# Queries before keys and values in a hybrid encoder layer, each query tile stored head by head, with the output projection's first operands loaded before the values

## The chip, the cores and the metric

One core of one Trainium2 chip runs the whole kernel. The core has a tensor engine (TensorE, PE in the profile; its weight loads are PEld), a vector engine (DVE), a scalar engine (ACT), a general engine (POOL) and a sync engine (SP), which here issues nearly all transfers. The metric is the device time of one execution in microseconds (us).

## The reference, cut to what matters

A two-layer encoder step. In each layer three groups of heads work on the same input: latent attention with 8 heads, an mLSTM with 4, a gated delta net with 4. Their outputs are gated, joined into 1536 mixed columns and projected back to 1024. A prompt of 16 + 1024 rows and 8 running streams of 16 rows each go through it, 1168 rows together. The change concerns the step between the input projection and the attention, where queries, keys and values are made from the normalised latents, and the beginning of the output projection.

```python
def mixer_layer(x, pos0, ...):
    proj = rms_norm(x, norm_w) @ w_in
    (c_q, c_kv, k_r, z_a, m_q, ...) = jnp.split(proj, ...)
    q = (rms_norm(c_q, q_norm) @ w_uq).reshape(B, L, MLA_HEADS, MLA_NOPE + MLA_ROPE)    # 8 heads of 64 + 32
    q_nope, q_rope = q[..., :MLA_NOPE], apply_rope(q[..., MLA_NOPE:], pos)
    c_new = rms_norm(c_kv, kv_norm)
    ...
    o_a = mla_attention(q_nope, q_rope, c_all, kr_all, w_uk, w_uv, ...)
    ...
    mixed = jnp.concatenate([o_a * jax.nn.silu(z_a), o_m * jax.nn.silu(z_m), o_g * jax.nn.silu(z_g)], axis=-1)
    return x + mixed @ w_out, ...

def mla_attention(...):
    k_nope = jnp.einsum('bkr,rhd->bkhd', c_kv, w_uk)
    v = jnp.einsum('bkr,rhd->bkhd', c_kv, w_uv)
    ...
        sc = jnp.einsum('blhd,bkd->bhlk', q_rope[:, s:e], k_rope[:, :n_keys])
        sc = sc + jnp.einsum('blhd,bkhd->bhlk', q_nope[:, s:e], k_nope[:, :n_keys])
        p = jax.nn.softmax(jnp.where(mask, sc * scale, -jnp.inf), axis=-1)
        o = jnp.einsum('bhlk,bkhd->blhd', p, v[:, :n_keys])
```

## The kernel before

**Number format.** A float32 product is made of three matmuls on a rounded high half and the remainder of each operand (`mm3`, L428 on). `split` makes the halves: a cast on ACT (line L421 in the trace), a subtraction on DVE or POOL in turn (L425). `weights` loads a weight tile through one buffer (`wf`) and splits it into one of two (`wh`).

**Memory.** Large tiles are pages, 28 buffers of 128 x 1200 float32 (`pg`, `free`); `room(n)` says whether n of them are free. PSUM has 3 buffers `pa`, for projections and transposes, and 5 `pb`, for scores and the rest. Small work tiles come from rings: "hp" has 3 buffers, "th" two. The "hp" ring is shared by the evicted queries and keys, by the loads of queries and keys for a head (`gload`) and by the loads of the mixed rows (`mixes`). Scratch for the queries (`qS`, 8 heads x 96 x 1168), the keys (`kS`, 4 pairs of heads x 128 x 1040) and the mixed rows (`mixS`, 12 x 128 x 1168) is in DRAM.

**Order of the work.** The program is written by generators that a planner (`Weave`) takes in turn, by a clock that it models from the matmuls (`W.t`). Threads (`prep`, `gload`, `att_s`, `att_t`, `att_fin`, and some for the running streams) yield a number, the microseconds after which they are due again, or a name, which they wait for. Where no thread is due and the pages suffice, the next step of a filler is written: input projection (`projs`), then `qkv`, `out_first`, `out_proj`. So the order on each engine is settled when the program is built; on the chip each engine takes its queue in that order, and waits there for what the next instruction needs. All loads and stores named here stand in SP's one queue, but for those of the rotary keys (`krS`), which POOL issues.

**The step in question.** `qkv` takes five weight tiles in the order keys, queries 0 and 1, values, queries 2 and 3, queries 4 and 5; the next tile is loaded when one is begun. Each query tile (27 matmuls) covers three slices of the 1168 rows, 400, 384 and 384. Tiles 0 and 3 hold the rotary parts of four heads each: DVE makes the products with the two tables (`tab`), one of 128 partitions (L1442) and two of 64 (L1445), POOL adds them. Tiles 1, 2, 4 and 5 hold the other 64 columns of two heads each and are scaled by ACT (L1451). Each slice is evicted into an "hp" buffer and stored from there, a rotary slice by two transfers [4 x 16 x 400], another by one [2 x 64 x 400]. Keys (12 pieces of 6 matmuls) are copied by ACT (L1425) into "hp" and stored piece by piece; values (9 tiles of 6) go to four pages by ACT and DVE in turn (L1411, L1414, L1415).

**Around it.** `gload` waits for `("spill", g)`, the queries and keys of a pair of heads, then loads a head's pieces back through "hp" and splits them (ACT L1506, POOL L1507). `att_s` makes scores and softmax (ACT L1553) for one head and 128 rows at a time, 9 such units per head in layer 0 and 8 in layer 1, at most four ahead of `att_t`, which transposes the weights (L356) and multiplies by the values. `out_first` starts the output projection with the first 4 of 12 mixed rows, which don't come from the attention: 24 slices of 12 matmuls, filler between the units. It loads the twelve operand pieces with `mixes`:

```python
        def mixes(k0, k1):
            mx = [(pg(F32R), pg(F32R)) for _ in range(k0, k1)]
            for s0, s1 in wsl:
                for k, (a, b_) in zip(range(k0, k1), mx):
                    t_ = wt("hp", 528, 3)[:, :s1 - s0]
                    ld(t_, mixS[k][:, s0:s1])
                    split(t_, a[:, s0:s1], b_[:, s0:s1])
            return mx
```

`wout` loads a weight tile of that projection (SP L1944 in one stretch, L437 in others). The matmuls themselves stand on L345, transposes on L356.

Of the kernel before, what the change touches and what calls it, by code (L numbers as in the profile page):

```python
# [294 lines left out]
def _build(nc, tc, ctx, I, O, layers):  # L295
# [275 lines left out]
    def layer(l, XH, XLp, XL, xres, xw, R):  # L571
# [795 lines left out]
        def qkv():  # L1367
# [7 lines left out]
            VV = A["VV"] = [pg() for _ in range(4)]  # L1375
            order = ["k", "q0", "v", "q1", "q2"]

            def load(i_):
                if i_ == len(order):
                    return None  # L1380
                t_ = order[i_]
                if t_ == "v":
                    return weights(I["wuv"][l].rearrange("p k c -> p (k c)"), 1024)
                if t_ == "k":
                    return weights(I["wuk"][l].rearrange("p g k c -> p (g k c)"), 1024)
                g = int(t_[1])
                return weights(I["wuq"][l, :, 2 * g:2 * g + 2].rearrange("p h k c -> p (h k c)"), 768)

            nxt = load(0)
            todo = [(i_, t_, j) for i_, t_ in enumerate(order)  # L1390
                    for j in {"v": (0,), "k": range(4)}.get(t_, [2 * (ord(t_[-1]) - 48), 2 * (ord(t_[-1]) - 48) + 1])]
            gr = 0
            ckn = []
            pre = -1
            for i_, t_, j in todo:
                if i_ != pre:
                    wh, wl = nxt
                    nxt = load(i_ + 1)
                    pre = i_
                if t_ == "v":  # L1400
                    for g in range(4):
                        gate(G.memset(VV[g][:, 1024:1152], 0.0))
                    for c in range(9):
                        ps = pa()
                        tc_ = slice(OFF[c], OFF[c] + 128)
                        for k in range(2):
                            mm3(ps, ckh[k][:, tc_], ckl[k][:, tc_], wh[:, 512 * k:512 * k + 512],
                                wl[:, 512 * k:512 * k + 512], k == 0, k == 1)
                        if c == 0:
                            for g in range(4):  # L1410
                                S.copy(VV[g][0:16, 1024:1152], ps[0:16, 128 * g:128 * g + 128])  # L1411
                        else:
                            o = 512 * ((c - 1) % 2)
                            (S.copy if c % 2 else V.tensor_copy)(VV[(c - 1) // 2][:, o:o + 512], ps)  # L1414
                        yield  # L1415
                elif t_ == "k":
                    w0 = 256 * j
                    for s0, s1 in KS:
                        ps = pa()
                        w = s1 - s0  # L1420
                        for k in range(2):
                            sl = slice(w0 + 128 * k, w0 + 128 * k + 128)
                            mm3(ps[:, :w], wh[:, sl], wl[:, sl], ckh[k][:, s0:s1], ckl[k][:, s0:s1], k == 0, k == 1)
                        t32 = wt("hp", 528, 3)
                        S.copy(t32[:, :w], ps[:, :w])  # L1425
                        QE.dma_start(kS[j][:, s0:s1], t32[:, :w])
                        yield
                else:
                    rope = j in (0, 3)
                    a = j // 3  # L1430
                    w0 = 384 * (j % 2)
                    for s0, s1 in SLICES:
                        ps = pa()
                        w = s1 - s0
                        for k in range(3):
                            sl = slice(w0 + 128 * k, w0 + 128 * k + 128)
# [564 lines left out]
```

## Time and profile before

| | |
|---|---|
| median of 3 runs | 2755.95 us (2751.81 to 4520.19) |
| the profiled execution's own time | 2758.32 us |
| its span in the trace | 2756.5 us |
| TensorE busy | 2570.4 us, 93% of the span, 18526 matmuls |
| DVE, ACT, POOL busy | 1524.6, 1181.5, 715.9 us |
| bytes moved, mean | 259.80 MB, 94 GB/s |

The span is the stretch from the first to the last instruction that the hardware profiler recorded; the execution's own time is 1.8 us longer. A busy matmul engine says that matmuls were in flight, not that they ran at the full clock: the granted clock stands apart, as a share of 2.4 GHz. Of the rows that a later section shows, each was taken from this one execution.

### The profile page before, as it was taken

What the parts mean: (1) busy time and instruction counts of PE and PEld (TensorE: products, weight loads), DVE (VectorE), ACT (ScalarE), POOL (GpSimd) and SP (SyncE); (2) the same over time, 40 slices, a digit from 0 to 9 for tenths busy, and PEclk for the clock granted to TensorE, in tenths of its full rate; (3) what the DMA queues carried; (4) which work ended last, traced back from release to release, by engine and by line L of the source; (5) the groups of instructions that cost most, each with busy time, mean ns of one, the idle gap of its engine ahead of it and who ended that gap; (6) DMA issues with size and microseconds to landing.
All of it is one profiled execution on the core that took longest, in us unless ns stands there. A gap on an engine that the chain in (4) does not pass through costs nothing. (4 is left out here: it accounts for less than half of the span.)

```text
span 2756.5 us, 48832 instructions
## 1 busy us (share of the span) xinstructions
PE 2570.4 (93%) x18526; PEld 2022.9 (73%) x18526; DVE 1524.6 (55%) x4280; ACT 1181.5 (43%) x2935; POOL 715.9 (26%) x803
## 2 busy tenths in 40 slices
PE   6999999999999689999999999999999976999997
PEld 4676777767767568879976767676776665788996
DVE  6568475564352255675566764756443413656746
ACT  4353444444442344464243534444443323545522
POOL 2223222122123232132341331222211322221414
PEclk9999999999999889999999999999999997999998
DMA  3212122221123243386422121212211333444852
GB/s 124 62 38 76 49 67 63 64 59 50 55 82 126 86 129 103 101 232 195 154 82 57 58 67 51 67 49 68 65 48 48 116 116 98 120 115 130 248 167 86
DMA packets 184538, 259.80 MB, mean 94 GB/s; under 512 B 50112, under 2 KB 143792, under 8 KB 184304
## 3 DMA queue, kind: packets, MB, share of 16 engines
q1 hardware_dynamic: 182576, 251.83, 30.7%
q0 software_dynamic: 1728, 4.86, 0.7%
q8 instruction: 146, 2.39, 0.4%
q14 instruction: 88, 0.72, 0.1%
HBM read 191.77 MB, written 64.86 MB: 93 GB/s over the span
## 5 line engine op out<-in xcount | busy, mean ns | idle before, releaser
L345 PE MATMUL pa<-pg,wh 128*128 128x384 f32 (+2 forms) x6324 | 1640.9, 391 | 44.3 <-ACT pg L421 17.6
L345 PEld LDWEIGHTS pa<-pg,wh 128*128 128x128 f32 x6324 | 1126.7, 196 | 84.3 <-issue 19.2
L345 PE MATMUL pa<-pg,wb 128*128 128x384 bf16 (+1 forms) x2208 | 750.1, 341 | 2.1 <-POOL pg L528 1.8
L345 PEld LDWEIGHTS <-wb 128*128 128x128 bf16 x2208 | 212.2, 97 | 355.3 <-issue 348.3
L345 PE MATMUL pb<-wk,pg 128*64 128x128 f32 (+5 forms) x3592 | 347.7, 261 | 10.1 <-DVE wk L1106 4.0
L345 PEld LDWEIGHTS pb<-wk,pg 128*128 128x128 f32 (+4 forms) x3592 | 279.8, 150 | 53.7 <-issue 31.6
L345 PE MATMUL pb<-pg,pg 128*128 128x128 f32 (+17 forms) x1508 | 288.2, 328 | 23.7 <-ACT pg L1553 14.2
L345 PEld LDWEIGHTS pb<-pg,pg 96*128 96x128 f32 (+5 forms) x1508 | 231.8, 195 | 48.0 <-ACT pg L1553 15.3
L425 POOL TENSOR_TENSOR wh<-wf,wh 128x1024 fp32r<-128x1024 f32 (+1 forms) x61 | 146.9, 2408 | 413.8 <-ACT wh L421 385.0
L421 ACT CAST wh<-wf 128x1024 fp32r<-128x1024 f32 (+1 forms) x122 | 126.4, 1036 | 213.0 <-PE pa L345 198.0
L1553 ACT ACTIVATE pg<-pb,wk 128x348 f32<-128x348 f32 (+9 forms) x232 | 121.4, 531 | 108.7 <-DVE wk L1549 94.3
L356 PE MATMUL pa<-cst,pg 128*128 128x128 f32 (+1 forms) x856 | 137.2, 284 | 18.0 <-ACT wk L1451 13.1
L1507 POOL TENSOR_TENSOR pg<-wk,pg 96x346 fp32r<-96x346 f32 (+1 forms) x96 | 85.5, 897 | 216.7 <-ACT pg L1506 177.6
L356 PEld LDWEIGHTS pa<-cst,pg 128*128 128x128 f32 (+1 forms) x856 | 105.3, 145 | 34.6 <-ACT wk L1451 13.6
L1611 DVE COPY wk<-pa 128x512 f32<-128x512 f32 (+4 forms) x116 | 65.0, 561 | 116.3 <-PE pa L356 100.0
L1543 DVE TENSOR_REDUCE wk<-pb 128x1 f32<-128x328 f32 (+9 forms) x232 | 109.8, 488 | 30.1 <-PE pb L345 29.0
L345 PE MATMUL pb<-wk,wk 32*32 32x16 f32 (+6 forms) x1776 | 111.0, 216 | 13.2 <-DVE wk L1113 4.1
L850 DVE SCALAR_TENSOR_TENSOR pg<-pg,vec,pg 128x1192 f32<-128x1192 f32 x72 | 106.0, 1487 | 16.0 <-ACT pg L848 15.7
L425 DVE TENSOR_TENSOR wh<-wf,wh 128x1024 fp32r<-128x1024 f32 (+1 forms) x61 | 73.9, 1211 | 70.7 <-ACT wh L421 70.2
L1611 ACT COPY wk<-pa 128x512 f32<-128x512 f32 (+4 forms) x116 | 55.7, 483 | 110.3 <-PE pa L356 109.5
L675 ACT COPY pg<-pa 128x384 f32<-128x384 f32 (+1 forms) x108 | 51.9, 481 | 110.0 <-PE pa L345 109.0
L441 ACT CAST wb<-wf 128x1024 bf16<-128x1024 f32 x92 | 96.3, 1046 | 4.1 <-DMA wf<-win 4.0
(302 smaller groups left out, 3320.5 us busy)
## 6 DMA issues: line engine op xcount, KB each, us to landing
wf<-win SPq DMA_DIRECT2D x92, 512.0 KB
pg<-latT SPq DMA_DIRECT2D x32, 520.0 KB
pg<-latN SPq DMA_DIRECT2D x32, 512.0 KB
wf<-wout SPq DMA_DIRECT2D x24, 512.0 KB
wk<-mix SPq DMA_DIRECT2D x60, 192.0 KB
xa<-wk SPq DMA_DIRECT2D x40, 192.0 KB
mix<-pg SPq DMA_DIRECT2D x12, 584.0 KB
mix<-pg SPq DMA_DIRECT2D x12, 576.0 KB
```

The costliest lines, as they stand in the source:

```text
L345: W.last = P.matmul(out, lhsT, rhs, start=start, stop=stop)
L356: W.last = P.transpose(out, in_, idn)
L421: S.copy(hi, src)
L425: lo_eng.tensor_sub(lo, src, hi.bitcast(F32))
L441: S.copy(wb[:, :n], wf)
L675: S.copy(o[:, s0:s1], ps)
L850: V.scalar_tensor_tensor(y[:, :n], cb[:, j:j + n], vcol(l, "cw", 4 * ti + j), y[:, :n], op0=ALU.mult, op1=ALU.add)
L1507: G.tensor_sub(lo, t_, hi.bitcast(F32))
L1543: V.tensor_reduce((mx[:n, j:j + 1] if np_ > 1 else nb[:n]), ps[:n, :n1 - n0], axis=AX.X, op=ALU.min)
L1553: S.activation(Pp[:n, n0:n1], pss[j][:n, :n1 - n0], AF.Exp, scale=-1.0, bias=nb[:n], accum_out=dn[:n, j:j + 1] if np_ > 1 else den[:n])
L1611: (V.tensor_copy if turn % 2 else S.copy)(pt[:rows, :w], ps[:rows, :w])
```

## The change

In each layer `qkv` now makes all six query tiles first, then the keys, then the values. A query tile is evicted into a page of its own (`sg`), slice by slice, and stored when its three slices are there, head by head over all 1168 rows: a rotary tile by eight transfers [16 x 1168] (L1419), another by two [64 x 1168] (L1422). Each key tile goes to a page too, and its pieces are stored from there (L1443). Latents of the queries and tables are freed after the sixth query tile, and the pages of the values are taken then. After the keys and ahead of the values the first weight tile of the output projection (`A["w0"]`) and its twelve operand pieces (`A["mx0"]`, eight pages) are asked for; `out_first` begins with these. A pair of heads is ready for `gload` when its key tile is made, and the transposes of the attention (`att_t`) begin once all values are (`D1["v"]`). The matmuls, their operands and their number stay the same.

```diff
-            order = ["k", "q0", "v", "q1", "q2"]
...
+                if t_ == "o":
+                    return wout(0, *PARTS[0], 1024 // (128 * (PARTS[0][1] - PARTS[0][0])))
+                return weights(I["wuq"][l, :, 2 * t_:2 * t_ + 2].rearrange("p h k c -> p (h k c)"), 768)
...
             nxt = load(0)
...
+            for j in range(6):
+                if j % 2 == 0:
                     wh, wl = nxt
...
+                    nxt = load(j // 2 + 1 if j < 4 else "k")
...
+                while not room(1):
+                    yield "idle"
+                sg = pg()
...
+                for s0, s1 in SLICES:
...
+                    q32 = sg[:, s0:s1]
...
-                            for x_ in range(2):
-                                QE.dma_start(qS[4 * a:4 * a + 4, 64 + 16 * x_:80 + 16 * x_, s0:s1], q32[64 * x_:64 * x_ + 64])
...
-                            QE.dma_start(qS[2 * gr:2 * gr + 2, 0:64, s0:s1], q32)
...
+                if j in (0, 3):
+                    for h in range(4):
+                        for x_ in range(2):
+                            o = 64 * x_ + 16 * h
+                            QE.dma_start(qS[4 * (j // 3) + h, 64 + 16 * x_:80 + 16 * x_], sg[o:o + 16, :T])
+                else:
+                    for h in range(2):
+                        QE.dma_start(qS[2 * gr + h, 0:64], sg[64 * h:64 * h + 64, :T])
+                    gr += 1
+                free(sg)
+            free(*cqh, *cql, *tab)
+            D1["qs"] = 1
+            VV = A["VV"] = [pg() for _ in range(4)]
+            for j in range(4):
+                if j == 0:
+                    wh, wl = nxt
+                    nxt = load("v")
...
+                sg = pg()
...
+                    S.copy(sg[:, s0:s1], ps[:, :w])
+                    QE.dma_start(kS[j][:, s0:s1], sg[:, s0:s1])
+                    yield
+                free(sg)
+                D1["spill", j] = 1
+            wh, wl = nxt
+            A["w0"] = load("o")
+            while not room(2 * (PARTS[0][1] - PARTS[0][0])):
+                yield "idle"
+            A["mx0"] = mixes(*PARTS[0])
...
+            D1["v"] = 1
+            free(*ckh, *ckl)
...
         def att_t():
             pend = None
             turn = 0
+            yield "v"
...
         def out_first():
             k0, k1 = PARTS[0]
             nm_ = 1024 // (128 * (k1 - k0))
-            while not room(2 * (k1 - k0) + RF):
-                yield "idle"
-            nxt = wout(0, k0, k1, nm_)
-            mx = mixes(k0, k1)
+            nxt, mx = A.pop("w0"), A.pop("mx0")
```

How instructions stand on three engines in layer 0, before and after. In the rows `pa`, `pg`, `wk` and `wf` with a number are PSUM buffers, pages, work tiles and weight tiles of the program; wuq, wuk and wuv are the weights of queries, keys and values.

SP before, from the load of the third query weights to head 0's first load; `qS<-wk` are stores of query slices.

```order
L437 DMA wf_9303<-wuq 128x768
L1449 DMA qS<-wk_9219 4x16x400 x2
L1449 DMA qS<-wk_9237 4x16x384 x2
L1449 DMA qS<-wk_9255 4x16x384 x2
L1454 DMA qS<-wk_9273 2x64x400
L1454 DMA qS<-wk_9286 2x64x384
L1454 DMA qS<-wk_9299 2x64x384
L367 DMA pg_9323<-mix 64x4x128 x2
L367 DMA pg_9323<-mix 64x16
L367 DMA pg_9323<-mix 64x4x128 x2
L367 DMA pg_9323<-mix 64x16
L367 DMA wk_9336<-qS 96x348
```

SP after, from the load of the third query weights to the first key store:

```order
L437 DMA wf_9171<-wuq 128x768
L1419 DMA qS<-pg_9080 16x1168 x8
L1422 DMA qS<-pg_9134 64x1168 x2
L1422 DMA qS<-pg_9176 64x1168 x2
L1419 DMA qS<-pg_9213 16x1168 x8
L437 DMA wf_9267<-wuk 128x1024
L1422 DMA qS<-pg_9272 64x1168 x2
L1422 DMA qS<-pg_9309 64x1168 x2
L437 DMA wf_9350<-wuv 128x1024
L1443 DMA kS<-pg_9355 128x348
```

The loads of the gate pages and of head 0 no longer follow the slices of a pair of heads at once; the stores of all six tiles stand together, and the key weights (wuk) behind the second rotary tile's eight.

DVE before, at the first rotary tile (pg_9065 and pg_9066 are the tables):

```order
L1442 SCALAR_TENSOR_TENSOR wk_9219<-pa_9209,pg_9065 128x400
L1445 SCALAR_TENSOR_TENSOR wk_9220<-pa_9209,pg_9066 64x400 x2
L1442 SCALAR_TENSOR_TENSOR wk_9237<-pa_9227,pg_9065 128x384
L1445 SCALAR_TENSOR_TENSOR wk_9238<-pa_9227,pg_9066 64x384 x2
L1442 SCALAR_TENSOR_TENSOR wk_9255<-pa_9245,pg_9065 128x384
L1445 SCALAR_TENSOR_TENSOR wk_9256<-pa_9245,pg_9066 64x384 x2
```

DVE after, at the same tile and the next rotary one:

```order
L1404 SCALAR_TENSOR_TENSOR pg_9080<-pa_9081,pg_9065 128x400
L1404 SCALAR_TENSOR_TENSOR pg_9080<-pa_9096,pg_9065 128x384
L1404 SCALAR_TENSOR_TENSOR pg_9080<-pa_9111,pg_9065 128x384
L1407 SCALAR_TENSOR_TENSOR wk_9091<-pa_9081,pg_9066 64x400 x2
L1407 SCALAR_TENSOR_TENSOR wk_9106<-pa_9096,pg_9066 64x384 x2
L1407 SCALAR_TENSOR_TENSOR wk_9121<-pa_9111,pg_9066 64x384 x2
L1404 SCALAR_TENSOR_TENSOR pg_9213<-pa_9214,pg_9065 128x400
L1407 SCALAR_TENSOR_TENSOR wk_9224<-pa_9214,pg_9066 64x400 x2
```

The products of 64 partitions, which stood behind the first product of their own slice, now stand behind the first products of all three slices.

ACT before, at the first values (pg_9070 to pg_9073 are their pages, pa_9312 the first tile's PSUM buffer):

```order
L1451 ACTIVATE wk_9299<-pa_9289 128x384
L1411 COPY pg_9070<-pa_9312 16x128
L1411 COPY pg_9071<-pa_9312 16x128
L1411 COPY pg_9072<-pa_9312 16x128
L1411 COPY pg_9073<-pa_9312 16x128
L1414 COPY pg_9070<-pa_9338 128x512
L1414 COPY pg_9071<-pa_9358 128x512
L1414 COPY pg_9072<-pa_9378 128x512
L1506 CAST pg_9334<-wk_9336 96x348
L1506 CAST pg_9330<-wk_9356 64x348
```

ACT after, at the first values (pages pg_9346 to pg_9349; the casts of wk are splits of mixed operands):

```order
L421 CAST pg_9503<-wk_9511 128x400
L421 CAST pg_9505<-wk_9515 128x400
L421 CAST pg_9507<-wk_9519 128x400
L421 CAST pg_9509<-wk_9523 128x400
L1465 COPY pg_9346<-pa_9574 128x512
L421 CAST pg_9503<-wk_9527 128x384
L1462 COPY pg_9346<-pa_9563 16x128
L1462 COPY pg_9347<-pa_9563 16x128
L1462 COPY pg_9348<-pa_9563 16x128
L1462 COPY pg_9349<-pa_9563 16x128
```

Casts of the operand pieces now stand ahead of and between the copies of the values.

## Rows read from the trace of the kernel before

**Rows 1.** The page: the span, and busy time, share and instructions of engines.

```profile
span 2756.5 us, 48832 instructions
...
PE 2570.4 (93%) x18526; PEld 2022.9 (73%) x18526; DVE 1524.6 (55%) x4280; ACT 1181.5 (43%) x2935; POOL 715.9 (26%) x803
```

**Rows 2.** Windows: stretch, length, busy time and instructions by engine, clock, DMA.

```profile
857.20:1001.32 144.12, 105.73 (x555) 91.12 (x554) 43.94 (x120) 49.48 (x125) 37.82 (x46) 0.86 0.40 117
2204.57:2354.41 149.84, 108.80 (x553) 92.47 (x552) 45.72 (x115) 48.95 (x123) 39.64 (x47) 0.83 0.38 113
1001.32:1179.50 178.18, 176.20 (x1363) 146.95 (x1362) 109.50 (x385) 84.78 (x259) 39.44 (x45) 1.00 0.36 99
1180.00:1200.00 20.00, 17.71 (x171) 14.03 (x167) 13.81 (x54) 11.02 (x41) 1.24 (x8) 1.00 0.91 268
```

**Rows 3.** Waits of PE, layer 0, 857 to 1003: total us, times, longest.

```profile
PE pa L345 <- ACT pg L421: 8.3, 1, 8.3
PE pb L345 <- ACT pg L1553: 7.7, 2, 5.7
...
PE pa L345 <- ACT wk L1451: 5.7, 4, 3.2
PE pa L345 <- ACT pg L1414: 5.2, 1, 5.2
```

**Rows 4.** Timeline of PE, layer 0: start, us, instructions, idle time before and releaser.

```profile
857.20 6.01 PE L345 MATMUL pa<-pg,wh 128*128 128x348 f32 x36
...
868.61 12.69 PE L345 MATMUL pa<-pg,wh 128*128 128x348 f32 x72 [0.65 <-ACT wk L1425]
...
887.12 10.00 PE L345 MATMUL pa<-wh,pg 128*128 128x512 f32 x42 [0.34 <-ACT wk L1451]
...
903.91 8.86 PE L345 MATMUL pa<-pg,wh 128*128 128x384 f32 x36 [5.16 <-ACT pg L1414]
...
1001.32 1.09 PE L345 MATMUL pb<-wk,pg 128*64 128x128 f32 x16
```

**Rows 5.** Chain of waits, layer 1: start, us, what.

```profile
2208.57 2.98 DMA kS<-wk
...
2259.00 7.09 DMA qS<-wk
...
2266.69 9.44 DMA qS<-wk
...
2319.96 6.63 DMA wk<-mix
...
2343.12 3.29 DMA wk<-mix
```

**Rows 6.** Timeline of DVE, layer 0.

```profile
819.70 1.23 DVE L425 TENSOR_TENSOR wh<-wf,wh 128x1024 fp32r<-128x1024 f32 x1 [4.05 <-ACT wh L421]
...
873.48 0.57 DVE L1442 SCALAR_TENSOR_TENSOR wk<-pa,pg 128x400 f32<-128x400 f32 x1 [13.77 <-PE pa L345]
874.06 1.16 DVE L1445 SCALAR_TENSOR_TENSOR wk<-pa,pg 64x400 f32<-64x400 f32 x2
```

**Rows 7.** SP: the query stores (ns least, median, most), a weight load's issue.

```profile
L1449 SPq DMA_DIRECT2D qS<-wk x24: 502/511/703, 876.4 to 2279.8; - x24
...
1337.62 0.38 SPq L1944 DMA_DIRECT2D wf<-wout  x1
```

**Rows 8.** Timeline of ACT, layer 0.

```profile
972.20 1.05 ACT L421 CAST pg<-wk 128x400 fp32r<-128x400 f32 x2 [6.33 <-DMA wk<-mix]
...
989.97 0.51 ACT L421 CAST pg<-wk 128x384 fp32r<-128x384 f32 x1 [1.21 <-DMA wk<-mix]
...
1341.29 1.05 ACT L421 CAST pg<-wf 128x1024 fp32r<-128x1024 f32 x1 [4.92 <-DMA wf<-wout]
```

**Rows 9.** Timeline of POOL, layer 0.

```profile
972.80 1.04 POOL L425 TENSOR_TENSOR pg<-wk,pg 128x400 fp32r<-128x400 f32 x1 [4.52 <-ACT pg L421]
```

**Rows 10.** DMA issues: times, KB each, median us from issue to landing.

```profile
pg<-krS POOLq DMA_DIRECT2D x32, 130.0 KB, 3.6
```

More of the change, by code (lines that the diff above doesn't have):

```diff
@@ L1374, in qkv, with load @@
             ckh, ckl, cqh, cql = A["ckh"], A["ckl"], A["cqh"], A["cql"]
-            VV = A["VV"] = [pg() for _ in range(4)]
-            order = ["k", "q0", "v", "q1", "q2"]
[L1378 to L1381, printed above, removed]
+            def load(t_):
                 if t_ == "v":
@@ new lines, in qkv @@
+            D1["qs"] = 1
[4 more added lines that the diff above has]
+                    nxt = load("v")
+                while not room(1):
+                    yield "idle"
+                sg = pg()
+                w0 = 256 * j
+                for s0, s1 in KS:
+                    ps = pa()
+                    w = s1 - s0
+                    for k in range(2):
+                        sl = slice(w0 + 128 * k, w0 + 128 * k + 128)
+                        mm3(ps[:, :w], wh[:, sl], wl[:, sl], ckh[k][:, s0:s1], ckl[k][:, s0:s1], k == 0, k == 1)
+                    S.copy(sg[:, s0:s1], ps[:, :w])
+                    QE.dma_start(kS[j][:, s0:s1], sg[:, s0:s1])
+                    yield
+                free(sg)
+                D1["spill", j] = 1
@@ new lines, in qkv @@
+            wh, wl = nxt
+            A["w0"] = load("o")
+            while not room(2 * (PARTS[0][1] - PARTS[0][0])):
+                yield "idle"
+            A["mx0"] = mixes(*PARTS[0])
+            for g in range(4):
+                gate(G.memset(VV[g][:, 1024:1152], 0.0))
+            for c in range(9):
+                ps = pa()
+                tc_ = slice(OFF[c], OFF[c] + 128)
+                for k in range(2):
+                    mm3(ps, ckh[k][:, tc_], ckl[k][:, tc_], wh[:, 512 * k:512 * k + 512],
+                        wl[:, 512 * k:512 * k + 512], k == 0, k == 1)
+                if c == 0:
+                    for g in range(4):
+                        S.copy(VV[g][0:16, 1024:1152], ps[0:16, 128 * g:128 * g + 128])
+                else:
+                    o = 512 * ((c - 1) % 2)
+                    (S.copy if c % 2 else V.tensor_copy)(VV[(c - 1) // 2][:, o:o + 512], ps)
+                yield
```

89 lines of the change are left out of this document (18 added, 71 removed).

## The prediction, made before the changed kernel ran

> **What bounds the kernel now.** The page comes first: TensorE (PE) is busy for 93% of a span of 2756.5 us [rows 1], so time is to be had only where PE stands still or runs at the lower of its two clock levels. The page's strip of slices shows two such places, one per layer, and the windows measure them [rows 2]. Their columns are the stretch, its length, busy time of PE, weight loads, DVE, ACT and POOL, and PE's granted clock. In layer 0 the stretch goes from the first key matmul (857.20) to head 1's first value product (1001.32, [rows 4]): PE is busy for 105.73 of 144.12 us, idle for 38.4, and at a granted clock of 0.86 the busy part loses up to 0.14 x 105.73 = 14.8 us more. In layer 1 it is 41.0 idle and 0.17 x 108.80 = 18.5. Together 112.7 us, 4.1% of the time: that is all that the change can win. Right behind the stretch PE is busy for 176.20 of 178.18 us at clock 1.00, so what is saved ahead of it isn't swallowed there; it reaches the end of the layer.
>
> Then the waits of PE in layer 0 [rows 3]: behind L421 (splits of the projection's operands), L1553 (the softmax), L1451 and L1414 (evictions of queries and values). No such engine is full; they wait for DMAs. The chain of waits names these [rows 5]: query stores of 200 and 192 KB take 7.09 and 9.44 us, where a key store of 174 KB takes 2.98. The evicted slice lies in one of three "hp" buffers, held until its store has landed; loads of queries, keys and projection operands use the same three, and all of them stand in SP's one queue. A slow store thus stops the eviction, that PE's PSUM buffer, and the loads behind it.
>
> **The change, part by part.**
>
> Matmuls: none is added or removed. The last six query slices of a layer move out of the attention, and the rest changes places before it. Dense rates are 6.01 / 36 = 0.167 us (348 columns), 12.69 / 72 = 0.176 (mostly 384) and 10.00 / 42 = 0.24 (512) [rows 4]. So six query tiles of 27 matmuls are 28.5 us (4.75 each), 72 matmuls of the keys 12, 54 of the values 13: some 54 us per layer in one piece, without attention between. What matters is what interrupts it now. I walk through it from 857.20 with the order of the changed program and the durations of this trace.
>
> (a) Query stores: 24 per layer before and after, but from a page, so no buffer waits. Gone with them are the waits on L1451 and most of L421's. In the changed order nothing but SP waits for them, and through SP the key weights (c).
>
> (b) First query tile. DVE does the three first products, 0.57 us each, before the pairs of half products, 1.16 a pair [rows 6]; the order shows that. The first PSUM buffer is free only after two more first products and a pair: about 863.8, while PE has done its three slices at 862.0. Cost **1.8 us**; the other rope tile goes slice by slice, 1.7 us on DVE against 1.6 on PE, and costs nothing.
>
> (c) Key weights. They are asked for behind the second rope tile's eight stores. That tile leaves PE at 878.0, DVE and POOL (1.04 an operation of that width, [rows 9]) at 881.0; eight issues at a median of 0.51 us and a short gap each, 4.5 in all, end at 885.5 [rows 7]. A weight load of 512 KB then lands in 3.7 us (1337.62 to 1341.29, [rows 7, 8]), here behind 600 KB of stores, so I take 4.5; cast 1.05 and remainder 1.23 follow [rows 6, 8]. Keys start at 892.3 instead of 887.5: **4.8 us**. The nearest idle time of that size, 5.16 us, was followed by 36 matmuls in 8.86 us where the dense rate gives 6.35 [rows 4]: **2.5 us** for the clock. Bounds: nothing, if the stores are issued and land early; 8 us if the load waits for all of them.
>
> (d) Values. ACT's order puts the copy of the first value tile behind the casts of five mixed operands, whose loads come after the last key store on SP. With three buffers the fourth load waits for the first split: load 3.29 us [rows 5], cast 0.52, remainder 1.04, then the same again and one more cast: the copy ends some 11.5 us after the keys. PE has three value tiles and a score piece, some 5 us, until it needs that PSUM buffer: **6.5 us**, and **1.5** for the clock (less than in (c), since the next copies wait anyway). All twelve casts took from 972.20 to 990.5, 1.5 us each [rows 8]; at that pace the last key piece of head 0, behind the twelve loads on SP, is ready 25 us after the keys; PE is there after 6.5 + 1.5 + 13 and stands for **4 us**. Bounds: 3 us for all, if loads land in 2.98; the upper one is a rival.
>
> (e) Start of attention: the first scores, softmax and transposes have the projection's matmuls beside them, ready at last. The order has 84 of those ahead of head 1's first value product where it had 36. I take **4 us** for small waits, between 0 and the 7.7 of L1553 [rows 3].
>
> (f) End of attention: six query slices (9.7 us) no longer fill it, and 48 matmuls of the projection (8.5 us) are used up at its start, so the projection ends before the attention does. The nearest unfilled stretch is 1180 to 1200, PE 17.71 of 20 us [rows 2], 11% idle: on 18 us that is 2, and I take **2.5 us**; bounds 0 and 5.
>
> (g) Pages: the mixed operands hold eight pages from the values on, the stored tiles one at a time. The order shows head 1's loads well ahead of its scores, 30 us of PE work earlier, so the next late thing is not a page.
>
> Sum per layer of what is lost in the changed kernel: 1.8 + 7.3 + 8 + 4 + 4 + 2.5 = 27.6, in both 55. Gain 112.7 - 55 = 57.5 us. The profiled execution took 2758.3 us (span 2756.5 and 1.8 around it): 2700.8, and since the median of the runs is 2.4 below it, **2698 us**. What is within 2% (2701 to 2811) a measurement hardly tells from no change, and the forecast lies on that border.
>
> **A rule against the change.** The sixteen-partition stores of 75 KB [16 x 1168] take the place of six of 100 KB a tile. The nearest row is a load of 32 partitions, 130 KB: 3.6 us to landing [rows 10]; eight overlapping cost SP's issue time only, eight in a row 29 us.
> The Trainium skill, "DMA: Bandwidth & Descriptors", section "Rules for kernel authors", says that two transfers to separate partition halves serialize and advises one wide transfer. By that rule the price would be the one of rival 3; no row here shows two query stores in a row at their own pace.
>
> **The rivals.**
> 1. Better than forecast (0.13): loads land in 2.98 us once the slow stores are gone, the clock doesn't fall, the start and the end of the attention cost 3 us together. For it speaks that 6.63 us for an operand load was measured amid slow stores, against it ACT's order. Loss 1.8 + 3 + 3 + 3 = 10.8 per layer: 2758.3 - 91 - 2.4 = 2665.
> 2. Operand loads stay slow (0.18), 6.63 us as measured [rows 5], since twelve of them now share the queue with the key stores and head 0's loads. A load and its split take 8.2 us, over three buffers 2.7 each instead of 1.5: 15 us more for twelve and 3.5 for the clock, per layer. Gain 57.5 - 37 = 20: 2736.
> 3. The small stores go one after another (0.07): 29 us instead of 4.5 before the key weights, 24 us per layer: gain 9, 2747. Against it: key stores are issued one behind the other too, and one lands in 2.98 [rows 5].
> 4. Slower (0.06): the values wait for ACT, ACT for an operand, its load for a buffer whose split stands behind a value copy, so that one load is in flight at a time. Each then costs its whole 6.63 + 1.6 us, twelve 99 us instead of 18: 81 more per layer, where the gain was 28.7, so 52 lost in each: 2860. It decides from 3.9 us a load on (28.7 / 12 + 1.5).
> That the moved order doesn't take effect is excluded by the order of the built program.
>
> **How the numbers follow.** The forecast has 0.56, with 2675 to 2725 as its own range from the bounds in (c) to (f); 0.35 of it lies below 2701, 0.21 above. Faster by over 2%: 0.13 + 0.35 = 0.48. Within 2%: 0.21 + 0.18 + 0.07 = 0.46. Slower by over 2%: 0.06. The range from 2665 to 2747 ends on rivals 1 and 3; left out are rival 4 and the far half of either, 0.06 + 0.065 + 0.035 = 0.16.
>
> **What would show it.** Query stores that land in about 3 us and no wait for them on ACT (a); a gap of 4 to 6 us ahead of the first key matmul, at low clock behind it (c); one of about 6 us after the third value tile, with ACT waiting for an operand (d); the twelve casts within 18 us; idle time of both stretches together down from 79 to about 42 us. Wrong would be: operand loads of 5 us and more (rival 2), key weights landing after 895 counted from the same start (rival 3), or idle time in the attention's last two heads above 8 us.

## The result and the profile after

The changed kernel takes 2719.82 us (median of 4 runs, 2717.3 to 2721.77) where the kernel before takes 2753.94: 0.9878 of it, 95% interval 0.9859 to 0.9898. Run again later beside other kernels it gave 0.9891 (0.9869 to 0.9913). The gain is 34 us by the medians; the forecast, 2698, had 56. The interval reaches 0.2% to either side, so 1.2% is clear of no change here, where the prediction drew that border at 2%.

The page of the profiled execution, as in [rows 1]:

```profile
span 2715.5 us, 48753 instructions
...
PE 2561.5 (94%) x18526; PEld 2020.6 (74%) x18526; DVE 1520.2 (56%) x4280; ACT 1181.8 (44%) x2935; POOL 708.2 (26%) x803
```

This execution took 2717.3 us, 41.0 less than the one of before. To see where they went, the step and all behind it is cut in two per layer: from the first matmul of the step to the first load of a running stream's cached latents (the planner asks for these when the attention's last head is loaded), and from there to the first projection weights of layer 1, or to the end. Windows of the changed kernel (columns as in [rows 2]):

```profile
852.46:1155.16 302.70, 279.39 (x1921) 237.23 (x1920) 155.72 (x504) 134.76 (x381) 77.98 (x95) 0.96 0.43 117
1155.16:1331.74 176.58, 162.44 (x1110) 153.14 (x1109) 101.56 (x208) 74.53 (x190) 51.79 (x66) 0.96 0.63 197
2186.45:2474.24 287.79, 267.56 (x1840) 229.56 (x1839) 146.22 (x450) 127.80 (x351) 77.17 (x94) 0.96 0.46 124
2474.24:2715.50 241.26, 214.78 (x1370) 199.11 (x1370) 141.89 (x294) 90.94 (x224) 75.17 (x91) 0.92 0.50 161
```

The same four of the kernel before, cut at the same events:

```profile
857.20:1182.41 325.21, 284.83 (x1954) 240.52 (x1954) 154.91 (x509) 135.43 (x386) 78.10 (x94) 0.94 0.38 107
1182.41:1350.63 168.22, 158.65 (x1077) 148.64 (x1076) 101.78 (x202) 73.46 (x185) 54.30 (x67) 0.97 0.68 209
2204.57:2530.96 326.39, 284.93 (x1912) 241.56 (x1912) 152.30 (x473) 133.59 (x369) 77.39 (x95) 0.92 0.37 106
2530.96:2756.50 225.54, 201.32 (x1299) 188.42 (x1298) 139.19 (x271) 85.02 (x207) 77.08 (x90) 0.94 0.55 177
```

The length less PE's busy time is its idle time. Layer 0 takes 302.70 + 176.58 = 479.3 us where it took 493.4, 14.1 less; layer 1 529.1 where it took 551.9, 22.9 less; the remaining 4 us lie outside the two layers' windows, where the code does the same, and where two profiles of the changed kernel differ by 3.4 us (the step begins at 852.46 and at 855.84). In the first windows of the layers idle time fell from 40.4 to 23.3 and from 41.5 to 20.2 us; in the second ones it rose, from 9.6 to 14.1 and from 24.2 to 26.5. (The cut goes by events: after the change 33 and 72 matmuls stand in the second windows that stood in the first ones.) Busy time, over all four, fell only from 929.7 to 924.2 us: the matmuls are the same, so this is all that the clock gave back.

The granted clock says where. One less the clock, times PE's busy time, added up over slices of 2 us, is what the clock costs: in the first windows 14.3 + 16.8 = 31.1 us before and 10.1 + 8.8 = 18.9 after, in the second ones 4.3 + 7.7 = 12.0 before and 6.4 + 13.4 = 19.8 after. The step gave 12.2 us of low clock back, and the end of the attention took 7.8 of them again.

Waits of PE in layer 0, 857 to 1003 us, those over 1.7 us; they answer to [rows 3]:

```profile
PE pa L345 <- ACT pg L1465: 4.7, 1, 4.7
PE pa L356 <- DVE wk L1901: 4.3, 1, 4.3
PE pa L345 <- ACT pg L1442: 4.2, 1, 4.2
PE pa L345 <- DVE wh L425: 3.8, 1, 3.8
PE pa L345 <- DVE wk L1407: 1.8, 1, 1.8
```

No wait is left for a query's eviction that a store holds up (the 1.8 us on L1407 are DVE's products for the first rotary tile), and none for the softmax. The timeline of PE gives them in order; it answers to [rows 4]:

```profile
852.46 5.07 PE L345 MATMUL pa<-pg,wh 128*128 128x400 f32 x27
859.34 25.73 PE L345 MATMUL pa<-pg,wh 128*128 128x400 f32 x135 [1.82 <-DVE wk L1407]
888.84 11.29 PE L345 MATMUL pa<-pg,wh 128*128 128x348 f32 x54 [3.77 <-DVE wh L425]
904.35 4.67 PE L345 MATMUL pa<-pg,wh 128*128 128x348 f32 x18 [4.22 <-ACT pg L1442]
...
914.51 0.75 PE L345 MATMUL pb<-pg,pg 96*128 96x348 f32 x3 [1.33 <-POOL pg L1510]
920.00 10.88 PE L345 MATMUL pa<-wh,pg 128*128 128x512 f32 x36 [4.73 <-ACT pg L1465]
```

Six query tiles in one piece (27 + 135 matmuls) with one gap of 1.82 us; then 3.77 for the key weights, 4.22 among the keys, 1.33 and 4.73 at the values. Behind these gaps the matmuls are slow: 54 of the keys in 11.29 us where the dense rate of [rows 4] gives 9.0, 18 in 4.67 for 3.0, 36 of the values in 10.88 for 8.6.

ACT in the same place:

```profile
886.48 1.04 ACT L421 CAST wh<-wf 128x1024 fp32r<-128x1024 f32 x1 [0.88 <-DMA wf<-wuk]
...
903.48 0.48 ACT L1509 CAST pg<-wk 96x348 fp32r<-96x348 f32 x1 [5.38 <-DMA wk<-qS]
903.86 1.13 ACT L1442 COPY pg<-pa 128x348 f32<-128x348 f32 x3
...
918.46 1.00 ACT L421 CAST pg<-wk 128x400 fp32r<-128x400 f32 x2 [1.82 <-DMA wk<-mix]
919.37 0.58 ACT L1465 COPY pg<-pa 128x512 f32<-128x512 f32 x1
```

The weights' cast follows its load at once. The cast at 903.48 is head 0's first query piece: ACT waits 5.38 us for its load, three finished key pieces behind it; that is the gap of 4.22. The copy at 919.37 is the first value tile, behind two casts of mixed operands.

SP, and the page of DMA issues (KB each, median us from issue to landing):

```profile
878.73 3.56 SPq L1419 DMA_DIRECT2D qS<-pg  x8
882.33 0.42 SPq L437 DMA_DIRECT2D wf<-wuk  x1
```

```profile
mix<-pg SPq DMA_DIRECT2D x12, 584.0 KB, 5.3
...
qS<-pg SPq DMA_DIRECT2D x16, 292.0 KB, 3.8
...
qS<-pg SPq DMA_DIRECT2D x32, 73.0 KB, 2.0
```

Eight small stores are issued in 3.56 us and land in 2.0 us each, the larger ones in 3.8 (medians). The first line is a store of another stage, [128 x 1168] in one transfer, which is of use below. The store that took 7.09 or 9.44 us in [rows 5] is gone.

The end of the attention has new waits, one of 5.12 us for the very last unit:

```profile
1181.84 0.23 PE L356 MATMUL pa<-cst,wk 16*64 16x16 f32 x1 [5.12 <-DVE wk L1636]
...
1195.60 0.97 PE L356 MATMUL pa<-cst,pg 128*128 128x128 f32 x4 [2.77 <-ACT pg L1783]
```

and PE's granted clock falls there, to 0.83 and in layer 1 to 0.62, where the kernel before had 0.89 over 30 us of its layer 0 (1180 to 1210) and 0.83 over 20 us of its layer 1 (2540 to 2560). The changed kernel first (PE is busy for all of the last stretch), then the kernel before:

```profile
1180.00:1210.00 30.00, 24.71 (x150) 23.91 (x151) 19.29 (x33) 13.03 (x32) 11.96 (x22) 0.83 0.79 234
2450.00:2480.00 30.00, 26.22 (x198) 21.42 (x199) 20.60 (x71) 17.05 (x53) 6.64 (x10) 0.91 0.47 124
2480.00:2500.00 20.00, 20.00 (x118) 15.64 (x117) 11.03 (x38) 9.07 (x31) 1.64 (x3) 0.62 0.13 35
```

```profile
1180.00:1210.00 30.00, 25.67 (x198) 20.49 (x195) 23.69 (x65) 16.13 (x50) 9.94 (x18) 0.89 0.94 277
2540.00:2560.00 20.00, 16.98 (x94) 14.04 (x95) 17.84 (x36) 12.74 (x35) 8.34 (x11) 0.83 0.92 296
```

### The profile page after: what moved, and what is told of

It is laid out like the page before. It is cut to its first block, busy times and chain, and to the rows that moved or that the text cites. A ratio compares the mean times of both kernels' runs of the same rounds, so it can differ in the third digit from the quotient of the medians.

```text
span 2715.5 us, 48753 instructions
## 1 busy us (share of the span) xinstructions
PE 2561.5 (94%) x18526; PEld 2020.6 (74%) x18526; DVE 1520.2 (56%) x4280; ACT 1181.8 (44%) x2935; POOL 708.2 (26%) x803
## 5 line engine op out<-in xcount | busy, mean ns | idle before, releaser
L345 PEld LDWEIGHTS pa<-pg,wh 128*128 128x128 f32 x6324 | 1126.3, 196 | 63.3 <-issue 18.9
L345 PE MATMUL pb<-pg,pg 128*128 128x128 f32 (+16 forms) x1508 | 281.8, 324 | 15.4 <-DVE pg L425 4.0
L1546 DVE TENSOR_REDUCE wk<-pb 128x1 f32<-128x348 f32 (+9 forms) x232 | 110.1, 488 | 34.2 <-PE pb L345 32.6
```

The costliest lines, as they stand in the source:

```text
L345: W.last = P.matmul(out, lhsT, rhs, start=start, stop=stop)
L1546: V.tensor_reduce((mx[:n, j:j + 1] if np_ > 1 else nb[:n]), ps[:n, :n1 - n0], axis=AX.X, op=ALU.min)
```

## The experiments

Ratios are to the kernel before, run beside each. Idle and busy time are PE's, summed over the four windows, cut in each kernel at the same events. The last column is the part of the busy time that the clock cost, added up over slices of 2 us as above. Without it the busy time is 882 to 887 us in every kernel but one (907 with 54 matmuls more per layer), so where busy times differ at equal work, it is the clock. Two profiles of the changed kernel differ by 6.3 us in that column, and four kernels that end the attention alike (changed, changed again, heads held, key weights early) lose between 11 and 25 us in the second windows, so one profile's figure there is rough.

| kernel | ratio, 95% interval | idle us | busy us | of it clock, us |
|---|---|---|---|---|
| before | 1 | 115.6 | 929.7 | 43.1 |
| changed | 0.9878 (0.9859 to 0.9898) | 84.2 | 924.2 | 38.7 |
| changed, again | 0.9891 (0.9869 to 0.9913) | 82.4 | 929.8 | 45.0 |
| heads held | 0.9836 (0.9817 to 0.9855) | 74.5 | 920.9 | 38.8 |
| key weights early | 0.9867 (0.9850 to 0.9885) | 80.1 | 915.3 | 28.0 |
| operands behind the values | 0.9854 (0.9834 to 0.9875) | 74.7 | 927.5 | 44.0 |
| 54 matmuls more per layer | 0.9895 (0.9878 to 0.9913) | 74.8 | 940.3 | 33.0 |
| wide stores | 1.0109 (1.0087 to 1.0131) | 130.7 | 929.1 | 43.1 |
| before, stores by head | 0.9855 (0.9840 to 0.9871) | 78.5 | 921.4 | 34.0 |
| two late query tiles | 0.9855 (0.9829 to 0.9881) | 70.2 | 926.7 | 41.6 |
| two late tiles, heads held | 0.9791 (0.9774 to 0.9807) | 67.8 | 910.3 | 24.6 |
| three edits, no late tile | 0.9910 (0.9897 to 0.9923) | 83.4 | 929.3 | 46.1 |
| four late tiles, heads held | 0.9799 (0.9786 to 0.9812) | 59.9 | 916.5 | 30.3 |

**What the shape of the stores is worth, in the changed kernel.** The pages and the order stay, the stores go back to the shape of before:

```diff
-                    for h in range(4):
-                        for x_ in range(2):
-                            o = 64 * x_ + 16 * h
-                            QE.dma_start(qS[4 * (j // 3) + h, 64 + 16 * x_:80 + 16 * x_], sg[o:o + 16, :T])
+                    a = j // 3
+                    for x_ in range(2):
+                        QE.dma_start(qS[4 * a:4 * a + 4, 64 + 16 * x_:80 + 16 * x_], sg[64 * x_:64 * x_ + 64, :T])
...
-                    for h in range(2):
-                        QE.dma_start(qS[2 * gr + h, 0:64], sg[64 * h:64 * h + 64, :T])
+                    QE.dma_start(qS[2 * gr:2 * gr + 2, 0:64], sg[:, :T])
```

> The changed kernel (0.988 of before), but each query tile is stored from its page by wide transfers, two [4 x 16 x 1168] for a rotary tile and one [2 x 64 x 1168] for another, as the slices were stored before. Theory: it is the shape of these stores that makes them slow (192 KB in 9.44 us, 200 KB in 7.09, where a key store of 174 KB takes 2.98), and what is queued behind them waits even though no buffer does: at those rates 29 us for each of four tiles and 11 for each half of the rotary ones, so the key weights come 20 to 50 us late in each layer: 1.005 to 1.025 of before. Rival: the page alone took the stores off the path and their shape is indifferent: 0.985 to 0.990.

It takes 2777 us, slower than before. The chain of waits in layer 0 (start, us, what):

```profile
872.28 15.45 DMA wf<-wuk
...
902.02 28.19 DMA qS<-pg
```

One store [2 x 64 x 1168] lands after 28.19 us, and the key weights take 15.45 us where the changed kernel has 4.1 (882.33 to 886.48). It is not the size: the store [128 x 1168] above has the same 584 KB, stands in the same queue and lands in 5.3 us. A window of the wide variant in which PE stands and such stores are in flight has the reason in its last column but one, the mean busy share of the 16 DMA engines:

```profile
906.00:914.00 8.00, 0.00 (x0) 0.00 (x0) 0.00 (x0) 0.00 (x0) 0.00 (x0) 0.50 0.13 51
```

0.13 is two engines of 16, and from 896 to 902 it is the same. SP shows a second effect:

```profile
890.69 11.23 SPq L437 DMA_DIRECT2D wf<-wuv  x1
...
903.32 16.96 SPq L1441 DMA_DIRECT2D kS<-pg  x3
```

An issue that takes 0.3 to 0.5 us elsewhere holds SP for 11.23 us, three key stores for 16.96: SP can't get past its own issues, and all loads behind them start late. PE pays it with three gaps:

```profile
889.33 10.91 PE L345 MATMUL pa<-pg,wh 128*128 128x400 f32 x51 [5.93 <-ACT pg L1411]
919.51 7.33 PE L345 MATMUL pa<-pg,wh 128*128 128x346 f32 x30 [19.26 <-ACT pg L1440]
935.48 5.57 PE L345 MATMUL pa<-pg,wh 128*128 128x348 f32 x18 [8.64 <-ACT pg L1440]
```

The first theory holds, in size too: a page alone, with the new order and the prefetch, doesn't bring the gain; it loses 1% without the new shape.

**The shape alone, in the kernel before.**

```diff
-                            for x_ in range(2):
-                                QE.dma_start(qS[4 * a:4 * a + 4, 64 + 16 * x_:80 + 16 * x_, s0:s1], q32[64 * x_:64 * x_ + 64])
+                            for h in range(4):
+                                for x_ in range(2):
+                                    o = 64 * x_ + 16 * h
+                                    QE.dma_start(qS[4 * a + h, 64 + 16 * x_:80 + 16 * x_, s0:s1], q32[o:o + 16])
...
-                            QE.dma_start(qS[2 * gr:2 * gr + 2, 0:64, s0:s1], q32)
+                            for h in range(2):
+                                QE.dma_start(qS[2 * gr + h, 0:64, s0:s1], q32[64 * h:64 * h + 64])
```

> The kernel before, with nothing changed but the query stores of a slice: a rotary slice goes by eight transfers [16 x 400], another by two [64 x 400]. Theory: the slow stores held the three shared buffers; in 3 us each they free them, the waits of PE on query evictions (13 us in layer 0) and part of those on operand splits (8.3) go, 10 to 20 us per layer: 0.985 to 0.993 of before. Rival: the buffers are few and SP's queue is full, and 36 issues more per layer, 16 us of SP's time, take the gain back: 0.998 to 1.005.

0.9855: all of the gain of the whole change, with three shared buffers and the old order. Its stores (KB each, median us to landing), and PE's largest waits in layer 0:

```profile
qS<-wk SPq DMA_DIRECT2D x32, 96.0 KB, 2.2
...
qS<-wk SPq DMA_DIRECT2D x64, 24.0 KB, 1.6
```

```profile
PE pb L345 <- ACT pg L1556: 9.7, 3, 6.9
PE pa L345 <- ACT pg L421: 4.9, 1, 4.9
PE pa L345 <- ACT wk L1453: 4.3, 4, 1.8
```

The kernel before, in the row that [rows 3] leaves out:

```profile
PE pa L356 <- ACT wk L1451: 7.2, 1, 7.2
```

Where a store of 192 KB took 9.44 us, two of 96 take 2.2 each; the waits for query evictions are 4.3 us, where the kernel before had 5.7 [rows 3] and 7.2 more ahead of transposes. The further issues don't show (48 per layer, since two-head slices have one more each, which the expectation left out). What stays is the wait for the softmax. The rival falls.

**The waits that the change brought.** Three edits of the changed kernel, each taking away one gap. Heads held until all keys are made:

```diff
                 free(sg)
+            for j in range(4):
                 D1["spill", j] = 1
```

> The changed kernel (2720 us), but heads are loaded only when all four key tiles are made. Theory: the wait of the key copies (4.2 us in layer 0, 2.9 in layer 1) comes from head 0's first cast, which stands among the key copies on ACT and waits for its load; without it there the wait goes and the clock stays up, some 8 us in both layers: 2712. Rival: head 0's pieces are then late, the wait moves to the first scores (1.3 and 2.0 us now) and grows there by as much: 2718 to 2724.

0.9836, some 0.5% or 13 us below the changed kernel. The timeline of PE:

```profile
890.15 14.31 PE L345 MATMUL pa<-pg,wh 128*128 128x348 f32 x72 [3.74 <-DVE wh L425]
...
915.65 10.50 PE L345 MATMUL pa<-wh,pg 128*128 128x512 f32 x36 [7.03 <-ACT pg L1466]
```

The gap among the keys is gone, 72 matmuls in one piece. The wait at the values grows from 4.73 to 7.03, and the first scores wait 1.89 us for 1.33, so part of the gap moved. Yet idle time fell by 9.7 us in all: the theory holds, with a gain above its 8 us.

Key weights asked for ahead of the second rotary tile's stores:

```diff
-                    nxt = load(j // 2 + 1 if j < 4 else "k")
+                    nxt = load(j // 2 + 1) if j < 4 else nxk
...
+                if j == 3:
+                    nxk = load("k")
```

> The changed kernel, but the key weights are asked for ahead of the second rotary tile's eight stores (3.6 us of issues on SP). Theory: the 3.8 us ahead of the first key matmul fall to under 1 and the clock behind it stays up, 4 to 6 us per layer: 2710. Rival: keys that start earlier wait longer for ACT, whose cast for head 0 waits for a load that doesn't come earlier; the gap among the keys grows from 4.2 to 8 us: 2718 to 2722.

0.9867, not to be told from the changed kernel. The gap falls from 3.77 to 2.77 us only, though SP asks for the weights at 875.31, before the stores. ACT shows why:

```profile
887.97 0.49 ACT L1411 ACTIVATE pg<-pa 128x384 f32<-128x384 f32 x1 [1.08 <-PE pa L345]
888.36 1.04 ACT L421 CAST wh<-wf 128x1024 fp32r<-128x1024 f32 x1
```

The cast stands behind the last query tile's scales in ACT's order, and starts only then. Once the load is early, the cast's place is the next late thing; with its 1.04 us and the remainder's 1.23 behind it, the gap can't go below. My theory named the wrong half of the step; the rival's growing gap among the keys didn't come either (3.40 us, 4.22 before).

Operands behind the values, as in the kernel before:

```diff
-            A["w0"] = load("o")
-            while not room(2 * (PARTS[0][1] - PARTS[0][0])):
-                yield "idle"
-            A["mx0"] = mixes(*PARTS[0])
...
-            nxt, mx = A.pop("w0"), A.pop("mx0")
+            while not room(2 * (k1 - k0) + RF):
+                yield "idle"
+            nxt = wout(0, k0, k1, nm_)
+            mx = mixes(k0, k1)
```

> The changed kernel, but the output projection's first weights and its twelve operand pieces are loaded behind the values, as in the kernel before. Theory of the prediction, step (d): the waits at the values (4.7 us on a copy behind operand casts, 1.3 on the first score) go, but in their place the attention starts without filler until the pieces are there, 8.3 us in the kernel before: 2724, no gain from the prefetch beyond 4 us and no loss. Rival 1, the prefetch is worth much: 2735 and more. Rival 2, it costs more than it brings: 2712 or less, and more filler is left for the end of the attention, whose idle time falls.

0.9854: the wait at the values falls from 4.73 to 0.90 us, and the attention's start pays 2.63 and 1.41 for the operands. In size that is rival 2, some 8 us better, with intervals that just overlap; but the end of the attention idles as before (13.9 and 26.0 us), so the rival's reason isn't seen. What is sure is that the prefetch isn't worth 4 us.

**Filler for the end of the attention.** First, matmuls whose result nobody uses, behind the 24 slices:

```diff
+            for s0, s1 in wsl * 2:
+                yield from mixmm(pa(), s1 - s0, wh[:, o:], wl[:, o:], mx[:3], s0, s1)
```

> The changed kernel with 54 matmuls more per layer, whose result is thrown away, as filler behind the first 24 slices of the output projection: 9.5 us of dense work per layer, 19 in both. Theory: the end of the attention lost 8 us per layer and more because the filler is used up by then (six query slices left it); then the extra work lies in idle time, and the time stays within 2714 to 2726. Rival: the end is held up by something else (loads for the running streams, PSUM buffers), filler would not help, and the extra work adds: 2735 to 2740.

0.9895: 19 us of dense work cost 1 to 5, by which of the two runs of the changed kernel is taken. Busy time rises by 16.1 us, idle time falls by 9.4, and the second windows are as before the change: idle 8.2 and 23.7 us. The theory holds.

Then true filler: query tiles 4 and 5 behind the values, on top of the edit that puts the operands there. The key weights are asked for two tiles earlier with it.

```diff
-            for j in range(6):
+            def qtile(j, gr, wh, wl):
...
+            for j in range(4):
+                if j % 2 == 0:
+                    wh, wl = nxt
+                    nxt = load(1 if j == 0 else "k")
+                yield from qtile(j, (0, 0, 1, 2)[j], wh, wl)
+            free(*tab)
...
+            nxt = load(2)
...
             D1["v"] = 1
             free(*ckh, *ckl)
+            wh, wl = nxt
+            for j in (4, 5):
+                yield from qtile(j, j - 2, wh, wl)
+                D1["spill", j - 2] = 1
```

> As the kernel with the operands behind the values (0.985 of before), and the last two query tiles are made behind the values too, so that they are filler for the attention; the key weights are then asked for ahead of the query stores. Theory: the end of the attention loses 26 and 41 us there where the kernel before lost 14 and 36, because six slices of filler are gone; given back they take most of that and 3 us ahead of the keys: 0.978 to 0.981. Rival: filler only moves, the stretch of keys and values loses what the end gains, or page and queue waits for the late tiles eat it: 0.984 to 0.988.

0.9855, where the same without late tiles has 0.9854: the rival's number. The second windows fall to 8.2 and 23.2 us of idle time as the theory says, but the first ones rise by 2.7 and 1.3, and PE waits 8.3 us for a key copy. That wait is the one behind head 0's cast, so the next kernel holds the heads:

```diff
-                if j < 2:
-                    D1["spill", j] = 1
+            D1["spill", 0] = D1["spill", 1] = 1
```

> The same with the first two heads held until all four key tiles are made. Theory: the 3 to 4 us in which key copies wait behind head 0's cast go as they did when all heads were held, 0.002 to 0.004 better than the kernel that it changes. Rival: late query slices already cover that wait, and heads that start later cost as much: the same within 0.001.

0.9791: 0.0064 below the kernel that it changes, where the theory gave 0.002 to 0.004, and the best of all. Its windows:

```profile
854.30:1139.63 285.33, 272.97 (x1921) 231.64 (x1920) 153.63 (x504) 135.77 (x381) 78.91 (x95) 0.97 0.45 124
1139.63:1318.40 178.77, 164.61 (x1118) 154.51 (x1118) 101.87 (x209) 74.65 (x190) 51.65 (x66) 0.95 0.61 194
2171.77:2449.96 278.19, 264.64 (x1840) 226.57 (x1839) 146.06 (x450) 128.96 (x351) 77.66 (x94) 0.97 0.46 128
2449.96:2685.80 235.84, 208.09 (x1370) 193.58 (x1370) 141.46 (x294) 90.78 (x224) 75.69 (x91) 0.95 0.51 165
```

Idle time of the first windows is 12.4 and 13.6 us, where the changed kernel has 23.3 and 20.2, and busy time is 13.9 us less at the same work, since the clock cost 24.6 where it cost 38.7. Its second windows, though, idle as long as the changed kernel's (14.2 and 27.8 us): the late tiles were used up ahead of them, at the start of the attention. So they help here, but not where the theory put it. The same edits without the late tiles, and with the key weights early:

> The changed kernel with three edits together: heads held until all key tiles are made, operands behind the values, key weights ahead of the second rotary tile's stores; all six query tiles first. Theory (the late tiles are what made the best kernel so far, 0.979, as filler for the attention): 0.983 to 0.986, and the end of the attention loses 22 us or more in layer 0. Rival (these three edits alone make it, the late tiles add nothing): 0.978 to 0.981.

0.9910, worse than each of its three edits alone, so they don't add. When the heads are held and the operands come late, nothing is ready as the values end; PE waits 7.4 us in five pieces for operand splits there. Query tiles in that place have their operands in SBUF already. That is 1.2% between two kernels that differ in this and in how early the key weights come; the first is the cause by the waits, and it wasn't tried alone. With four late tiles, ones that use weights 1 and 2:

> The best kernel so far (0.979) with four query tiles behind the values in place of two, the order of the kernel before but for the first two query tiles ahead of the keys. Theory: more filler is left for the end of the attention, which lost 22 and 38 us there and 14 and 36 before: 0.975 to 0.978. Rival: its slices displace those of the output projection, and the later loads wait for tiles that come late: 0.979 to 0.985.

0.9799: the same as with two, within the intervals. Idle time is the lowest of all, 59.9 us, and the end is at 8.8 and 23.3 as expected, but busy time is 6.2 us longer. The clock took the gain back in this profile: it cost 30.3 us for 24.6. That is about what two profiles of one kernel differ by, so whether it belongs to the kernel stays open.

The control, the changed kernel once more:

> The changed kernel unaltered, beside the others on one chip: 0.988 of before within 0.002. Were the order, the pages and the prefetch worth something beyond the shape of the stores, it would have to be below the 0.9855 that the kernel before gave with its stores by head alone; the theory now is that it isn't.

0.9891, above the 0.9855 of the kernel before with its stores by head; the intervals just touch (0.9869 and 0.9871).

## Why the prediction was right in its sign and its waits, and wrong in a size

**What bounds the kernel.** Right, and shown: slow query stores held it. In the kernel before ACT waited 34.2 us in all for them to free a buffer, and SP was held too, 6.41 us for two of them at 2260.76 and 7.54 for four at 2268.05; what part each of the two ways had is not shown. In the wide variant, with no buffer held, it was SP's queue. The prediction read them off the chain [rows 5], but it credited the page with the gain, "24 per layer before and after, but from a page, so no buffer waits". The runs part the two: the new shape without the page gives 0.9855, the page without the shape 1.0109. The shape was in the sum only through faster loads in (c) and (d).

The Trainium skill, "DMA: Bandwidth & Descriptors", section "Why a DMA increments its semaphore by 16 and not by 1", says that a transfer runs on as many engines as the largest number up to 16 that divides the outermost dimension above 1 of both its sides. By that a store [2 x 64 x 384] has two engines and one [64 x 1168] sixteen. The traces agree: the share of 0.13 above is two of 16 engines, and in size 200 KB in 7.09 us, 192 in 9.44 and 584 in 28.19 are 20 to 28 KB a microsecond for an outermost 2, 292 KB in 3.8 are 77 for 64.

**(a)** holds: no wait for a query store is left. **(b)** 1.82 us for 1.8. **(c)** The gap is 3.77 for 4.8, the clock behind it 2.3 for 2.5; the bound, all stores landing first, was far off, since they land in 2.0 and 3.8 us. **(d)** 4.73 + 1.33 = 6.1 us for 6.5, and the place, a value copy behind operand casts on ACT, is right; the twelve casts take from 913.95 to 930.4, 16.5 us for 18. The 4 us that I had for the last key piece at the scores didn't come there; in their stead head 0's first cast stopped the key copies, 4.22 and 2.92 us, which the sum didn't have; that the waits add up so well is in part luck. **(e)** The softmax waits are gone; one wait of 4.3 us for the projection's adding on DVE (L1901) takes their place, as long as the 4 us taken. DVE itself waits ahead of it 1.15 us for the softmax and 0.35 for a load of input rows; what else made it late is not shown.

**The step that failed** is the clock in the sum. The prediction took the losses at low clock, 14.8 + 18.5 = 33.3 us, and left 4 of them per layer, so 25.3 were to come back; (e) and (f) had none. The 33.3 were near the mark (31.1 by slices). Idle time over the four windows fell by 31.4 us, where its part of the forecast, 57.5 - 25.3, was 32.2. Busy time fell by 5.5 (and by nothing in the second profile). Two things went wrong. In the first windows the clock still cost 10.1 and 8.8 us where the sum left 4 each, so 12.2 came back and not 25.3: behind the gap of 1.82 us, 135 matmuls took 25.73 where 0.176 each gives 23.8, 1.9 more, and behind the next three 2.3 + 1.7 + 2.3; in all 8.2 us in layer 0. The second profile agrees, 10.3 and 9.6. And at the end of the attention, where the sum had nothing, the clock cost 19.8 us (25.1 in the second profile) where it had cost 12.0: up to 0.17 x 24.71 = 4.2 us in the stretch of layer 0 shown above and 0.38 x 20 = 7.6 in layer 1, up to 2.8 and 2.9 in the two of the kernel before.

**(f)** was too small with it: 2.5 us per layer, where idle time of the second windows rose by 4.5 and 2.3 and the clock cost the above. The sign that was to show it wrong, over 8 us of idle time in the last two heads, came in layer 0: PE is busy for 49.94 of 58.65 us there (1123.74 to 1182.39), 8.7 us idle; in layer 1 it is 3.8 (2414.93 to 2480). Filler was the reason as stated: 54 further matmuls put the idle time back to 8.2 and 23.7 us.

**(g)** holds as far as the trace goes: no wait for a page was among PE's.

**The rivals.** The third, small stores that go one after another, is out: eight issued in 3.56 us, each landing in 2.0. The rule of the Trainium skill that the prediction weighed with it ("DMA: Bandwidth & Descriptors", section "Rules for kernel authors"), to use one wide transfer, is the wrong way round for this shape, since the kernel with the wide ones takes 2.3% longer (1.0109 against 0.988). Rival 2 had loads that stay slow: the loads of [128 x 400] operands take 5.6 us in the median, those of 384 columns 3.3, so its sign, 5 us and more, came for the first kind, but the twelve casts kept their time. Rival 4 had one load in flight at a time; that wasn't seen.

In numbers: 37.0 us came from the two layers where 57.5 were forecast; 4.0 came from elsewhere; and the execution that was profiled lies 2.5 us below its median, where the forecast took 2.4 off, 4.9 together. 20.5 - 4.0 + 4.9 = 21.4 are, but for rounding, the 22 us between forecast and result. 2719.8 lies in the forecast's own range of 2675 to 2725, near its end.

What stays open is the price of the rest of the change. Order, pages and prefetch together add between nothing and 0.7% to the time of the kernel with the new shape alone; which of them does, single edits don't tell, since they don't add up.

## What to carry to other kernels

Where a store or load takes several times as long as another of the same size, compare the shapes before the buffers: here an outermost dimension of 2 left two of 16 DMA engines at work. A store of 192 KB took 9.44 us where its halves take 2.2 each, one of 584 KB 28.19 where its halves take 3.8, and splitting them won all of the gain in place. When a change moves work forward out of a stage, ask what that stage has left to fill its waits, and whether what moves is needed there more. What low clock costs does not come back with closed gaps while others stay: here 47% of the idle time of the step went and 39% of what the clock cost there, where the prediction had counted on 76% (25.3 of 33.3 us); a gap of 1.82 us was still followed by 1.9 us of it, and in the profile two thirds of what came back was lost again at the end of the attention. So a clock loss is counted as won only where a whole stretch becomes dense.

## What the runs showed that was not expected

A slow transfer also stops the engine that issues: SP stood 11.23 us in one issue and 16.96 in three behind wide stores that hold no buffer. Two profiles of one kernel differ by 5.6 us in busy time with the same matmuls (924.2 and 929.8), as much as some of the edits move, and all of it is the clock (38.7 and 45.0 us). And three edits that each helped or did no harm (0.9836, 0.9854, 0.9867) gave 0.9910 together.
